# One encoder block on one core: modulation tiles redistributed over the stages, four diagonals for the row of silu(c), and each group's h computed inside the group before

## The chip, the cores and the metric

The kernel runs on one core of one Trainium2 chip. The metric is the time of one execution in microseconds on the device (us); before the change it is 1734.44 us, the median of three runs (1733.49 to 1734.98). Engine names are those of the profile: PE is the matmul engine and PEld its weight loads, DVE the vector engine, ACT the scalar engine, SP the queue that issues the transfers.

## What is computed

```python
mod = silu(c) @ w_ada + b_ada            # six vectors of 2048: sh1, sc1, gt1, sh2, sc2, gt2
h   = rmsnorm(x, g_pre_mix) * (1 + sc1) + sh1
y   = hybrid_mixer(h, ...)               # h @ w_in, a gated recurrence, window attention, w_a, w_b, w_out
x   = x + gt1 * rmsnorm(y, g_post_mix)
h   = rmsnorm(x, g_pre_ffn) * (1 + sc2) + sh2
y   = expert_choice_ffn(h, ...)          # 16 experts, each takes 32 of the 256 tokens
out = x + gt2 * rmsnorm(y, g_post_ffn)
```

There are 256 tokens and 2048 channels, all in float32. The weights make up nearly all of the 630 MB that are read, and each is used once.

## The kernel before

All weights come as tiles of 128 x 2048 floats (1 MB, 8 KB of each partition), and one list sets the order of the whole first part. This list, `prog`, is written out by hand (lines 227 to 264). Its entries are: `X` (load and normalise x), `A` and `B` (one tile of w_ada), `H` (make h for a group of the contraction), `W` (one tile of w_in), `YA`, `YB` and `O` (tiles of w_a, w_b and w_out). The transfers are issued by SP in exactly this order, and the experts' 384 tiles follow in `estream`. Every tile takes the slot that has been free for longest (`Mem.get`); there are 27 slots of 8 KB, four of which form a small ring for split weights (`hring`).

**Modulation.** `expand` (line 288) spreads silu(c), which lies over the partitions, into a row `CR` that every partition holds: for each of four blocks of 512, DVE writes a diagonal matrix (line 282), PE multiplies it by ones, and ACT copies the result (line 293). All four blocks use one buffer `diag`. `ada` (line 390) then multiplies a w_ada tile by `CR` and sums along the row, one DVE instruction per tile (line 392, called an *ada multiply* below). There are 96 of them: 32 `A` tiles (sh1 and sc1, needed for h) and 64 `B` tiles (the other four vectors, needed only in the last stage of the mixer and in the experts).

**Products.** A `W` tile is first split into a high and a low part (`split`: ACT casts in two halves at line 426, DVE subtracts at line 427), and then `prod` runs three products for each of its pieces; `finish` does this one tile behind the split (`LA = LAH = 1`). A tile of kind "t" takes 48 matmuls of 256 columns, one of kind "n" 24 of 512.

**Early groups.** Ten chunks of w_in (`EARLY`) are run in four groups, each over four of the 16 steps of the contraction, so that a group needs only eight `A` tiles. Between groups a chunk's sum is copied out of the accumulator (line 763) and in again (line 760). `("H", g)` stands at the head of each group. There the main loop (line 838) finishes all pending products, and then makes h for the group's four steps in `make_h` (lines 409 to 411, on ACT, ACT and DVE): the first half at once (`HK = 1`), the rest behind the split of the group's first tile. The `A` tiles of group g + 1 are mixed in after the second to the ninth tile of group g; in the last group 8 `B` tiles take their place (`BE = 8`).

**Late chunks, Y and O.** Eleven chunks (`LATE`, 44 tiles) are run one after the other, with 38 `B` tiles mixed in (`BL = 0.87`). Beside them `run_bg` works off the recurrence (`hgrn`, four parts) and then the attention (`attn_pre`, `attn`), four steps of these after each tile. Then come 16 tiles `YA` and `YB` and 16 tiles `O`, with the last 18 `B` tiles after the first 18 of these 32 (`BD = 18`). `router_consts` runs when the 48th `B` tile is done. Last come the router and the 16 experts.

Of the kernel before, what the change touches and what calls it, by code (L numbers as in the profile page):

```python
# [14 lines left out]
F32 = mybir.dt.float32  # L15
# [11 lines left out]
H = 8  # L27
# [3 lines left out]
EPS = 1e-6  # L31
ATT_SCALE = 128 ** -0.5
NEG = -3.0e38
BL = 0.87
BE = 8
BD = 18
NHL = 4
BG = 4
GRP = [4, 4, 4, 4]
NA0 = 1  # L40
HK = 1
LAH = 1


# [81 lines left out]
def block_kernel(ctx: ExitStack, tc: tile.TileContext, x, cols, pos, ident_in, hmask, smask, w_ada, w_in, w_a, w_b, w_out, w_r, w_gu, w_dn, out):  # L126
    nc = tc.nc
    V, S, E = nc.vector, nc.scalar, nc.tensor
# [3 lines left out]
    mem = Mem(sp, 27)  # L132
# [10 lines left out]
    def bank():  # L143
        ring["m"] = (ring["m"] + 1) % 3
        return PS[:, 2048 + 512 * ring["m"]:2560 + 512 * ring["m"]]
# [18 lines left out]
    pairs = []  # L164

    def latest(engine):
        for i in reversed(nc.cur_bb.bb.instructions):
            if i.engine == engine:
                return i
# [8 lines left out]
    def mm(o, l, r, start, stop, **kw):  # L178
        E.matmul(o, l, r, start=start, stop=stop, skip_group_check=True, **kw)  # L179
# [7 lines left out]
    def col(n, a=0, b=None):  # L187
        lo, hi = COLS[n]
        t, o = (ct0, 0) if lo < NCOL0 else (ct, NCOL0)
        return t[:, lo - o + a:(hi if b is None else lo + b) - o]  # L190
# [15 lines left out]
    def tiny(n):  # L206
        a = spos[0]
        spos[0] += n
        assert spos[0] <= SMW
        return small[:, a:a + n]  # L210

    def table(name="natural_log_exp_and_others"):

        S.preload_act_table_set(name)

    def rsqrt(ss, n):

        l, r, t, v = tiny(n), tiny(n), tiny(n), tiny(n)
        S.activation(l, ss, AF.Ln, scale=1.0 / D, bias=epsc)
        S.activation(r, l, AF.Exp, scale=-0.5)  # L220
        V.tensor_scalar(v, ss, 1.0 / D, EPS, ALU.mult, ALU.add)
        V.tensor_tensor(t, r, r, ALU.mult)
        V.scalar_tensor_tensor(t, t, -0.5, v, ALU.mult, ALU.mult)
        V.scalar_tensor_tensor(r, t, 1.5, r, ALU.add, ALU.mult)
        return r


    NG = len(GRP)
    G0 = [sum(GRP[:g]) for g in range(NG)]
    prog = [("X",)]  # L230
    a_tiles = [("A", p, k) for k in range(KT) for p in range(2)]
    b_tiles = [("B", p, k) for p in range(2, 6) for k in range(KT)]
    prog += a_tiles[:2 * GRP[0]]
    for g in range(NG):
        prog.append(("H", g))
        if g < NG - 1:
            todo = a_tiles[2 * G0[g + 1]:2 * G0[g + 1] + 2 * GRP[g + 1]]
        else:
            todo = b_tiles[:BE]
            b_tiles = b_tiles[BE:]  # L240
        nt, ne = len(todo), len(EARLY)
        for i, n in enumerate(EARLY):
            prog.append(("W", n, G0[g], GRP[g]))
            k = min(nt, (i + 1) * nt // (ne - NA0)) - min(nt, i * nt // (ne - NA0))
            prog += todo[:k]
            todo = todo[k:]
        prog += todo
    def mix(items, n, m):

        nonlocal prog, b_tiles  # L250
        n = min(n, len(b_tiles))
        for i, it in enumerate(items):
            prog.append(it)
            k = min(n, (i + 1) * n // m) - min(n, i * n // m)
            prog += b_tiles[:k]
            b_tiles = b_tiles[k:]

    late = [("W", n, 4 * q, 4) for n in LATE for q in range(4)]
    mix(late, int(BL * len(late) + 0.5), len(late))
    dlist = []  # L260
    for c in range(4):
        dlist += [("YA", c, q) for q in range(2)] + [("YB", c, q) for q in range(2)]
    dlist += [("O", c, q) for c in range(4) for q in range(4)]
    mix(dlist, len(b_tiles), BD)

# [14 lines left out]
    def spread(c4, w, b=None):  # L280

        V.tensor_tensor(w, ident[:, None, :].to_broadcast([128, 4, 128]),
                        c4[:, :, None].to_broadcast([128, 4, 128]), ALU.mult)
        b = bank() if b is None else b
        mm(b, ones, w.rearrange("p a b -> p (a b)"), True, True)
        return b

    def expand(c16, name):

        r = mem.get([D], F32, name)  # L290
        w = mem.get([4, 128], F32, "diag")
        for c in range(4):
            S.copy(r[:, 512 * c:512 * c + 512], spread(c16[:, 4 * c:4 * c + 4], w))  # L293
        mem.put(w)
        return r

# [5 lines left out]
    def hk(tl, kt):  # L302
        return tl[kt // 8][:, kt % 8, :]
# [3 lines left out]
    S.activation(sig, col("c"), AF.Sigmoid)  # L307
    V.tensor_tensor(sig, sig, col("c"), ALU.mult)
    CR = expand(sig, "crow")
    X = [mem.get([D], F32, "x") for _ in range(NT)]  # L310
    ssq = tiny(NT)

    def norm_x():
        for tt in range(NT):
            nc.sync.dma_start(X[tt], x[tt])
        scr = mem.get([D], F32, "sq")
        for tt in range(NT):
            S.activation(scr, X[tt], AF.Square, accum_out=ssq[:, tt:tt + 1])
        mem.put(scr)
        rs = rsqrt(ssq, NT)  # L320
        for k2 in range(8):
            if k2 % 2 == 0:
                for tt in range(NT):
                    xp = X[tt][:, 256 * k2:256 * k2 + 512]
                    S.activation(xp, xp, AF.Copy, scale=rs[:, tt:tt + 1])
            b = bank()
            for j in range(2):
                for tt in range(NT):
                    E.transpose(b[:, 256 * j + 128 * tt:256 * j + 128 * tt + 128],
                                X[tt][:, 128 * (2 * k2 + j):128 * (2 * k2 + j) + 128], ident)  # L330
            S.copy(NTl[k2 // 4][:, 2 * (k2 % 4):2 * (k2 % 4) + 2, :].rearrange("p a b -> p (a b)"), b)
        mem.put(*X)

# [56 lines left out]
    def ada(p, k, t):  # L390

        V.scalar_tensor_tensor(t, t, 1.0, CR, ALU.mult, ALU.mult, accum_out=MOD[:, p, k:k + 1])  # L392
        mem.put(t)

    def mod_gain(p, ks):
        m = MOD[:, p, ks]
        V.tensor_tensor(m, m, bada[:, p, ks], ALU.add)
        if p in (1, 4):
            V.scalar_tensor_tensor(m, m, 1.0, col("gpm" if p == 1 else "gpf")[:, ks], ALU.add, ALU.mult)
        elif p in (2, 5):  # L400
            V.tensor_tensor(m, m, col("gqm" if p == 2 else "gqf")[:, ks], ALU.mult)

    def make_h(g):
        ks = slice(G0[g], G0[g] + GRP[g])
        mod_gain(0, ks)
        mod_gain(1, ks)
        for kt in range(ks.start, ks.stop):
            n = hk(NTl, kt)
            S.activation(n, n, AF.Identity, scale=MOD[:, 1, kt:kt + 1], bias=MOD[:, 0, kt:kt + 1])
            S.copy(hk(HH, kt), n)  # L410
            V.tensor_tensor(hk(HL, kt), n, hk(HH, kt).bitcast(F32), ALU.subtract)
            if kt % 2:
                yield
        if g == NG - 1:
            mem.put(*NTl)
# [57 lines left out]
    def late_tiles(names):  # L473
        for n in names:
            OT[n] = mem.get([8, 256], F32R, n)
# [149 lines left out]
    def attn_pre():  # L625
        AQ, AKV = SL["AQ"], SL["AKV"]
        late_tiles(("BH", "BL"))
        V.memset(SC, NEG)
# [15 lines left out]
    def attn(h):  # L644
# [40 lines left out]
        S.copy(OT["BH"][:, h, :], b[:, :256])  # L685
        V.tensor_tensor(OT["BL"][:, h, :], b[:, :256], OT["BH"][:, h, :].bitcast(F32), ALU.subtract)
        yield
# [6 lines left out]
        "YA": (lambda k: OT["OH"][:, k, :], lambda k: OT["OL"][:, k, :]),  # L694
        "YB": (lambda k: OT["BH"][:, k, :], lambda k: OT["BL"][:, k, :]),
        "O": (lambda k: hk(MH, k), lambda k: hk(ML, k)),
# [51 lines left out]
    def finish(it, parts):  # L748
# [32 lines left out]
        elif k in ("YA", "YB"):  # L781
# [10 lines left out]
            if q == 1:  # L792
# [6 lines left out]
                else:  # L799
# [8 lines left out]
                    if c == 3:  # L808
                        table()
                        mem.put(OT["OH"], OT["OL"], OT["BH"], OT["BL"])  # L810
        else:
# [22 lines left out]
    last_b = [it for it in prog if it[0] == "B"][-1]  # L834
    LA = LAH
    pend = []
    hs = iter(())
    for it in prog:
        if it[0] == "H":
            while pend:  # L840
                finish(*pend.pop(0))
            hs = make_h(it[1])
            for _ in range(HK):
                next(hs)
            continue
        if it[0] == "X":
            norm_x()
            rotary()
            continue
        t = take()  # L850
        if it[0] in "AB":
            ada(it[1], it[2], t)
            if it[0] == "B" and it[2] % 4 == 3:
                mod_gain(it[1], slice(it[2] - 3, it[2] + 1))
            if it == last_b:
                mem.put(CR)
            if it == ("B", 4, KT - 1):
                router_consts()
        else:
            pend.append((it, split(t)))  # L860
            for _ in hs:
                pass
            while len(pend) > LA:
                finish(*pend.pop(0))
            run_bg(BG)
# [117 lines left out]
    for e in range(NE):  # L983
# [9 lines left out]
        for k in range(KT):  # L993
            w = take()
# [201 lines left out]
```

## Time and profile before

| | us |
|---|---|
| three runs: lowest, median, highest | 1733.49, 1734.44, 1734.98 |
| the profiled execution, its own time | 1734.13 |
| its span, first to last instruction | 1732.4 |
| PE, DVE, ACT busy | 1440.0, 777.0, 554.2 |
| read from HBM | 630.04 MB, 365 GB/s over the span |

A view by windows gives, for each stretch of the span, its length, the busy time of each engine with the number of its instructions, the granted clock of PE as a share of 2.4 GHz (PEclk; 0.50 is the lower level, 1.2 GHz), the busy share of the 16 DMA engines, and the rate. The time line lists instructions by start and duration, runs of equal ones merged (x2), with the idle time ahead of them and what ended it in brackets. Matmuls overlap one another, so PE's busy time is no measure of its pace.

### The profile page before, as it was taken

Reading aid. Unit: us, or ns where it says so; the run is one execution under the profiler, and the core shown is the slowest. Engines: PE = TensorE matmul, PEld = TensorE weight load, DVE = VectorE, ACT = ScalarE, POOL = GpSimd, SP = SyncE. Lnnn points to the kernel's source line nnn. Section 1 sums busy time; section 2 is a strip of 40 time slices with the busy share of each in tenths; the row PEclk is TensorE's granted clock in tenths of the full one; section 3 lists DMA queues with packets and bytes.
Section 4 is the critical chain, followed back from the end, with each engine's and each line's share of the span. In section 5 each row is a group of like instructions: output and inputs, shape, how many; then the busy total and the mean of one; then the engine's idle time right before and its main releaser. Section 6 shows DMA issues by size and latency. Waiting matters only on the chain.

```text
span 1732.4 us, 24211 instructions
## 1 busy us (share of the span) xinstructions
PE 1440.0 (83%) x10234; PEld 920.8 (53%) x10234; DVE 777.0 (45%) x1056; ACT 554.2 (32%) x854; POOL 0.2 (0%) x4
## 2 busy tenths in 40 slices
PE   4999999999999999997977767776777777777677
PEld 2989998789999999872422212321222222222123
DVE  6777787999997898443111101111111111111013
ACT  6467776665574444431200100000010000001013
POOL 0000000000000000000000000000000000000000
PEclk8999999999999999998998988888888887889797
DMA  9988955776978889867999999999999999999996
GB/s 384 418 342 320 361 209 217 275 298 247 355 305 341 336 349 371 334 249 292 419 419 420 419 419 419 419 419 419 419 420 420 419 419 419 420 419 419 419 420 243
DMA packets 88668, 633.72 MB, mean 366 GB/s; under 512 B 10096, under 2 KB 10480, under 8 KB 11760
## 3 DMA queue, kind: packets, MB, share of 16 engines
q1 hardware_dynamic: 88128, 631.39, 90.3%
q8 instruction: 80, 1.31, 0.3%
q10 hardware_dynamic: 432, 0.79, 0.1%
q14 instruction: 28, 0.23, 0.0%
HBM read 630.04 MB, written 2.10 MB: 365 GB/s over the span
## 4 chain that ended last, share of the span: by engine, by line
PE 48%; DMA 40%; DVE 6%; ACT 3%; issue 2%; SPq 0%; ACTq 0%; DVEq 0%
PE PS L179 47%; DMA w<-in_w_gu_dram 32%; DMA w<-in_w_dn_dram 7%; DVE w L392 2%; DVE hl L427 1%; ACT ew L1037 1%; DMA w<-in_w_in_dram 1%; ACT hl L426 0%; PE PS L1010 0%; DMA w<-in_w_ada_dram 0%; ACT ew L1007 0%; DVE F L500 0%; PE PS L889 0%; PE PS L678 0%; DVE T L506 0%
## 5 line engine op out<-in xcount | busy, mean ns | idle before, releaser
L179 PE MATMUL PS<-w,rt 128*32 128x512 f32 x2048 | 331.9, 724 | 149.7 <-DMA w<-in_w_gu_dram 148.3
L179 PE MATMUL PS<-hh,hl 128*128 128x256 f32 x2048 | 384.6, 288 | 13.8 <-ACT hl L426 8.9
L179 PE MATMUL PS<-hl,hl 128*128 128x256 f32 (+1 forms) x1184 | 357.0, 302 | 0.0
L179 PEld LDWEIGHTS PS<-hh,hl 128*128 128x128 f32 x2048 | 325.9, 194 | 16.3 <-ACT hl L426 9.3
L427 DVE TENSOR_TENSOR hl<-w,hl 128x1024 fp32r<-128x1024 f32 x232 | 281.4, 1223 | 117.3 <-ACT hl L426 117.0
L426 ACT CAST hl<-w 128x1024 fp32r<-128x1024 f32 x232 | 241.1, 1048 | 162.2 <-PE PS L179 155.0
L179 PEld LDWEIGHTS PS<-w,rt 128*32 128x32 f32 x2048 | 54.2, 117 | 387.6 <-DMA w<-in_w_gu_dram 329.7
L179 PEld LDWEIGHTS PS<-hl,hl 128*128 128x128 f32 x1184 | 229.1, 193 | 7.3 <-issue 1.0
L392 DVE SCALAR_TENSOR_TENSOR w<-w,crow 128x2048 f32<-128x2048 f32 x96 | 218.9, 2285 | 5.3 <-ACT crow L293 2.8
L179 PE MATMUL PS<-ew,rt 128*128 128x256 f32 x512 | 151.8, 422 | 59.8 <-ACT ew L1037 59.8
L1048 DVE TENSOR_TENSOR acc<-acc,PS 128x512 f32<-128x512 f32 x120 | 82.5, 688 | 258.6 <-PE PS L179 258.6
L179 PEld LDWEIGHTS PS<-ew,rt 128*128 128x128 f32 x512 | 91.5, 198 | 131.2 <-ACT ew L1037 117.8
L179 PE MATMUL PS<-w,ew 128*32 128x256 f32 x2048 | 146.9, 407 | 13.9 <-DVE ew L1016 13.9
L1037 ACT COPY ew<-PS 128x256 f32<-128x256 f32 x128 | 47.5, 371 | 250.9 <-PE PS L179 250.9
L1016 DVE TENSOR_TENSOR ew<-ew,PS 128x256 f32<-128x256 f32 x16 | 6.7, 421 | 234.4 <-ACT ew L1015 234.4
L949 DVE TENSOR_SCALAR rt<-ct,rt,small 128x32 f32<-128x32 f32 x32 | 9.4, 301 | 212.8 <-PE PS L179 212.8
L179 PE MATMUL PS<-hl,hh 128*128 128x512 f32 x320 | 101.8, 395 | 3.3 <-DVE hl L427 3.3
L179 PEld LDWEIGHTS PS<-w,ew 128*32 128x32 f32 x2048 | 56.1, 114 | 82.9 <-issue 44.0
L955 ACT COPY ew<-PS 128x512 f32<-128x512 f32 x15 | 8.8, 585 | 281.7 <-PE PS L179 281.7
L1007 ACT COPY ew<-PS 128x512 f32<-128x512 f32 x16 | 9.4, 585 | 235.6 <-PE PS L179 235.6
L179 PE MATMUL PS<-hl,mh 128*128 128x512 f32 x256 | 81.1, 397 | 0.8 <-ACT hl L426 0.7
L179 PEld LDWEIGHTS PS<-hl,hh 128*128 128x128 f32 x320 | 59.3, 188 | 17.0 <-DVE hl L427 5.0
(240 smaller groups left out, 1188.4 us busy)
## 6 DMA issues: line engine op xcount, KB each, us to landing
w<-in_w_gu_dram SPq DMA_DIRECT2D x256, 1024.0 KB, 19.9
w<-in_w_dn_dram SPq DMA_DIRECT2D x128, 1024.0 KB, 19.9
w<-in_w_ada_dram SPq DMA_DIRECT2D x96, 1024.0 KB, 7.2
w<-in_w_in_dram SPq DMA_DIRECT2D x84, 1024.0 KB, 7.3
w<-in_w_out_dram SPq DMA_DIRECT2D x16, 1024.0 KB, 9.2
w<-in_w_a_dram SPq DMA_DIRECT2D x8, 1024.0 KB, 6.4
w<-in_w_b_dram SPq DMA_DIRECT2D x8, 1024.0 KB, 7.6
x<-in_x_dram SPq DMA_DIRECT2D x4, 1024.0 KB, 6.1
```

Of the source, the lines that this page charges most:

```text
L179: E.matmul(o, l, r, start=start, stop=stop, skip_group_check=True, **kw)
L392: V.scalar_tensor_tensor(t, t, 1.0, CR, ALU.mult, ALU.mult, accum_out=MOD[:, p, k:k + 1])
L426: S.copy(hl[:, 0, :], w)
L427: V.tensor_tensor(hl[:, 1, :], w, hl[:, 0, :].bitcast(F32), ALU.subtract)
L949: V.tensor_scalar(oh[:, tt, :], io, pm3[:, tt, e:e + 1], r2[:, tt:tt + 1], ALU.is_equal, ALU.mult)
L955: S.copy(g, b)
L1007: S.copy(gu, b)
L1016: V.tensor_tensor(he, sl_, b3[:, :, 64:128], ALU.mult)
L1037: S.copy(EW[:, 2, 256 * (cb % 2):256 * (cb % 2) + 256], b[:, :256])
L1048: V.tensor_tensor(acc(cb), acc(cb), p3, ALU.add)
```

## The change

The list is built anew, the row of silu(c) gets four diagonal buffers, and h of the next group is made two steps at a time while the last two tiles of the group before are split.

```diff
-BL = 0.87
-BE = 8
-BD = 18
+BE = [0, 4, 4, 12]
+BL = 16
+BD = 27
-NA0 = 1
-HK = 1
+NA0 = 2
+NH0 = 3
...
     for g in range(NG):
-        prog.append(("H", g))
+        todo = b_tiles[:BE[g]]
+        b_tiles = b_tiles[BE[g]:]
         if g < NG - 1:
-            todo = a_tiles[2 * G0[g + 1]:2 * G0[g + 1] + 2 * GRP[g + 1]]
-        else:
-            todo = b_tiles[:BE]
-            b_tiles = b_tiles[BE:]
+            todo = a_tiles[2 * G0[g + 1]:2 * G0[g + 1] + 2 * GRP[g + 1]] + todo
         nt, ne = len(todo), len(EARLY)
         for i, n in enumerate(EARLY):
             prog.append(("W", n, G0[g], GRP[g]))
+            if g == 0 and i == 0:
+                prog.append(("H", 0))
             k = min(nt, (i + 1) * nt // (ne - NA0)) - min(nt, i * nt // (ne - NA0))
             prog += todo[:k]
             todo = todo[k:]
+
+            if g < NG - 1 and i == ne - NH0:
+                prog.append(("H", g + 1))
...
-    mix(late, int(BL * len(late) + 0.5), len(late))
+    mix(late, BL, len(late))
...
-        w = mem.get([4, 128], F32, "diag")
+        w = mem.get([4, 4, 128], F32, "diag")
         for c in range(4):
-            S.copy(r[:, 512 * c:512 * c + 512], spread(c16[:, 4 * c:4 * c + 4], w))
+            S.copy(r[:, 512 * c:512 * c + 512], spread(c16[:, 4 * c:4 * c + 4], w[:, c]))
...
     CR = expand(sig, "crow")
+    crow_done = latest(mybir.EngineType.Activation)
...
             S.activation(scr, X[tt], AF.Square, accum_out=ssq[:, tt:tt + 1])
+        pairs.append((latest(mybir.EngineType.Activation), crow_done))
...
-    hs = iter(())
+    hs, hg_ = iter(()), 0
     for it in prog:
         if it[0] == "H":
-            while pend:
-                finish(*pend.pop(0))
-            hs = make_h(it[1])
-            for _ in range(HK):
-                next(hs)
+            hs, hg_ = make_h(it[1]), it[1]
+            if it[1] == 0:
+                n, p = len(nc.cur_bb.bb.instructions), latest(mybir.EngineType.Activation)
+                for _ in hs:
+                    pass
+                pairs += [(i, p) for i in nc.cur_bb.bb.instructions[n:] if i.engine == mybir.EngineType.Activation]
             continue
...
             pend.append((it, split(t)))
-            for _ in hs:
-                pass
+            if it[0] == "W" and it[2] < G0[hg_]:
+                next(hs, None)
+            else:
+                for _ in hs:
+                    pass
```

`pairs` holds orderings within an engine: the first of a pair is placed behind the second. So the second square of x stands behind the last copy of `CR`, and the first group's h behind the casts of its first `W` tile.

Written out, the list has these numbers of w_ada tiles beside each stage's product tiles:

| stage (product tiles) | before | after |
|---|---|---|
| ahead of group 0 | 8 A | 8 A |
| groups 0, 1, 2, 3 (10 each) | 8 A, 8 A, 8 A, 8 B | 8 A, 8 A + 4 B, 8 A + 4 B, 12 B |
| late chunks (44) | 38 B | 16 B |
| YA and YB (16) | 16 B | 16 B |
| O (16) | 2 B | 12 B |

In the groups after the change the w_ada tiles follow the first eight product tiles, none the last two. Of the first 22 late tiles (the stretch in which the recurrence runs) 19 had a `B` tile before, and 8 have one after. The 48th `B` tile stands behind the second `YA`/`YB` tile before, and behind the twelfth after; the last one frees `CR` in stage O both times, behind its second tile before and its eleventh after.

## Rows read from the trace of the kernel before

**Rows 1.** Windows by stage: length, PE, PEld, DVE, ACT, POOL busy, PEclk, DMA share, GB/s.
```profile
104.00:277.00 173.00, 173.00 (x1300) 167.21 (x1301) 129.35 (x128) 127.70 (x144) 0.00 (x0) 0.99 0.79 302
277.00:441.00 164.00, 156.93 (x1027) 137.28 (x1026) 158.55 (x221) 97.41 (x133) 0.00 (x0) 0.99 0.68 257
441.00:518.00 77.00, 77.00 (x589) 74.19 (x589) 73.02 (x122) 49.08 (x100) 0.00 (x0) 1.00 0.83 321
588.00:688.00 100.00, 99.24 (x795) 96.93 (x794) 88.56 (x89) 42.95 (x43) 0.00 (x0) 1.00 0.92 362
688.00:773.00 85.00, 84.23 (x362) 67.60 (x362) 38.57 (x35) 34.24 (x44) 0.00 (x0) 1.00 0.76 294
...
720.00:763.00 43.00, 43.00 (x185) 34.39 (x184) 20.98 (x20) 19.56 (x25) 0.00 (x0) 1.00 0.56 194
790.00:805.00 15.00, 6.82 (x30) 2.23 (x34) 9.72 (x33) 1.33 (x4) 0.00 (x0) 0.56 0.26 108
...
850.00:1732.00 882.00, 641.22 (x4624) 216.82 (x4619) 133.94 (x236) 85.17 (x220) 0.00 (x0) 0.86 0.99 411
```

**Rows 2.** Time line of the start, all engines: from the first diagonal to the first product.
```profile
5.09 2.07 PE L179 MATMUL PS<-diag,ones 128*128 128x512 f32 x2 [5.09 <-DVE diag L282]
...
16.75 0.58 ACT L293 COPY crow<-PS 128x512 f32<-128x512 f32 x1 [2.33 <-PE PS L179]
...
17.37 2.29 DVE L392 SCALAR_TENSOR_TENSOR w<-w,crow 128x2048 f32<-128x2048 f32 x1 [2.77 <-ACT crow L293]
...
33.92 2.28 DVE L392 SCALAR_TENSOR_TENSOR w<-w,crow 128x2048 f32<-128x2048 f32 x1
...
36.70 1.09 ACT L409 ACTIVATE nT<-nT,MOD 128x256 f32<-128x256 f32 x2 [5.57 <-DVE MOD L399]
37.70 0.69 ACT L410 CAST hh<-nT 128x256 fp32r<-128x256 f32 x2
...
38.30 1.99 ACT L426 CAST hl<-w 128x1024 fp32r<-128x1024 f32 x2
...
39.39 0.58 PE L179 MATMUL PS<-hh,hl 128*128 128x256 f32 x1 [8.88 <-ACT hl L426]
```

**Rows 3.** DMA issues: the eighth w_ada tile and the first w_in tiles, issue and landing.
```profile
10.23 0.33 SPq L160 DMA_DIRECT2D w<-in_w_ada_dram  x1
...
w<-in_w_ada_dram SPq DMA_DIRECT2D x1, 1024.0 KB, 19.9
...
12.73 2.82 SPq L160 DMA_DIRECT2D w<-in_w_in_dram  x2
...
w<-in_w_in_dram SPq DMA_DIRECT2D x1, 1024.0 KB, 19.9
```

**Rows 4.** ACT's time line: groups 0 to 1 (99 to 118 us), then 1 to 2.
```profile
99.61 1.01 ACT L763 COPY Q<-PS 128x1024 f32<-128x1024 f32 x1
...
102.72 1.96 ACT L760 COPY PS<-F 128x1024 f32<-128x1024 f32 x2
...
111.31 1.01 ACT L763 COPY F<-PS 128x1024 f32<-128x1024 f32 x1 [1.89 <-PE PS L179]
...
157.04 1.01 ACT L763 COPY Q<-PS 128x1024 f32<-128x1024 f32 x1
...
162.48 1.02 ACT L763 COPY Q<-PS 128x1024 f32<-128x1024 f32 x1 [0.97 <-PE PS L179]
...
168.24 1.02 ACT L763 COPY F<-PS 128x1024 f32<-128x1024 f32 x1 [1.82 <-PE PS L179]
```

**Rows 5.** PE in the recurrence: products of 512 columns, then all matmuls touching the recurrence's tiles.
```profile
L179 PE MATMUL PS<-hl,hh 128*128 128x512 f32 x191 | 61.5, 399 | 3.3 <-DVE hl L427 3.3
...
L179 PE MATMUL PS<-hl,hl 128*128 128x512 f32 x95 | 38.0, 400 | 0.0
...
277.00:441.00 164.00, 33.85 (x248) 26.34 (x248) 42.29 (x92) 37.80 (x64) 0.99 0.68 257
```

## The prediction

> **What bounds the kernel now.** I read the windows by stage first, then the time line where a stage begins late, then matmul counts where a stage is slow. From 850 us to the end the DMA engines are 99% busy: the experts' transfers set the pace there, and the change does not touch them [rows 1]. From 790 to 805 us, while the router is worked out, DMA is only 26% busy: all free slots hold experts' tiles, and no slot comes free until PE starts on expert 0. So the end is the time at which PE gets there plus a fixed transfer, and whatever PE saves ahead of 805 us comes off the end one for one, as long as the slots are full by then.
>
> Ahead of that PE is the bound. From 104 to 277 us it is busy without a gap, likewise from 441 to 518 us, and nearly so from 588 to 773 us [rows 1]. Three places lose time. First the start: the first product begins at 39.39 us [rows 2]. Second the step from group 0 to group 1: the copies out of the accumulator stand 11.70 us apart (99.61 to 111.31 us), whereas from group 1 to 2 a tile of 512-column products takes 5.44 us and the next group's first tile 5.76 us, with nothing lost [rows 4]. Third the recurrence (277 to 441 us): DVE is busy for 158.55 of 164 us, and PE waits for it in turn [rows 1].
>
> **The change part by part.**
>
> *Start.* Four diagonal buffers take DVE's wait for PE out of the making of CR. From the first matmul pair at 5.09 us, four of 2.07 us back to back end at 13.4 us, and the last copy (0.58 us) at 14.0 us; now it ends at 17.3 us, with the first ada multiply at 17.37 us [rows 2]. The second square of x no longer stands between the copies. Seven multiplies and the small work between them take 33.92 − 17.37 = 16.55 us, so the eighth would start at 30.5 us. Its tile lands at 10.23 + 19.9 = 30.1 us [rows 3], just in time, and more could not be won. From there to h it is 36.70 − 33.92 = 2.8 us [rows 2]: the modulations are there at 33.3 us. The first w_in tile lands at 12.73 + 19.9 = 32.6 us [rows 3]; its casts (1.99 us [rows 2]), now put ahead of h, end at 34.6 us. One step of h is half of 1.09 and of 0.69 us [rows 2], which gives a first product at 35.5 us against 39.39 us, 3.9 us earlier. I take 3.5, because the low part of h now queues on DVE behind two subtractions. Bounds: 0, if the casts come later and hold up h, to 4.
>
> *From group 0 to group 1.* 11.70 − 5.76 = 5.9 us are lost [rows 4]. The chain is ACT's: h's casts, the second tile's casts and the copies back in (102.72 us) stand behind the copy out at 99.61 us, because the eighth A tile is multiplied only behind the split of the ninth tile. After the change the A tiles end one product tile earlier, nothing is flushed, and h is made behind the splits of the last two tiles. The step from group 1 to 2 shows that this suffices even with the old order. I take 5.9 (0 to 5.9). At the two later steps there is nothing to win.
>
> *Groups 1 to 3 get 12 more ada multiplies.* 12 x 2.29 = 27.5 us of DVE time. DVE goes from 129.35 to 156.8 of 173 us, 91% [rows 1]. Cover: PE. From 441 to 518 us DVE is busy for 73.02 of 77 us (95%) with PE gapless, and from 588 to 688 us for 88.56 of 100 us with PE at 99.24 [rows 1]. Transfers: at 411 GB/s a tile takes 2.55 us [rows 1]; 22 tiles in a group take 56.1 us, and PE needs 8 x 5.76 + 2 x 5.44 = 57.0 us. It fits, barely. I take a loss of 1 us; bounds 0 to 27.5, the case in which nothing is covered.
>
> *Late chunks lose 22.* In the recurrence it is 11 (19 less 8): 11 x 2.29 = 25.2 us of DVE, from 158.55 to 133 us [rows 1]. What this gives is what PE loses there now. In that window PE ran 191 + 95 = 286 matmuls of 512 columns, which is 11.9 tiles at 5.44 us, or 64.8 us. Of the 1027 matmuls 248 touch the recurrence's tiles; the remaining 493 are 10.3 tiles at 5.76 us, or 59.2 us [rows 1, 4, 5]. The 248 have a busy time of 33.85 us, the most that they can have held PE; their weight loads sum to 26.34 us, which I take as the least [rows 5]. So PE needed 150 to 158 of the 164 us, and lost 6 to 14. I take the middle, 10, and assume that nothing of it remains, since DVE would be at 133 of about 154 us (86%), below the 95% beside which PE has no gap. Bounds 0 to 14. The other 11 removed tiles lie beside a gapless PE and give nothing.
>
> PE's busy time reads differently: 156.93 of 164 us [rows 1] would leave 7.1 us to win, and the sum would come out at 1720. The Trainium skill (Perfetto Trace Analysis, Identifying the Most-Contended Engine) says that matmul busy time is no good measure, since these instructions are pipelined, and that weight-load busy time is better. The trace agrees: weight loads fall from 167.21 of 173 us to 137.28 of 164 us, far more than busy time does.
>
> *Stage O gets 10 more.* 22.9 us of DVE on 38.57 of 85 us makes 72% [rows 1]; cover: PE. Their transfers are 10 x 2.55 = 25.5 us; DMA idles for 0.44 x 43 = 19 us from 720 to 763 us and for 0.74 x 15 = 11 us from 790 to 805 us [rows 1], so 30 us take them in. The last B tile holds CR, one slot, for nine O tiles longer. The router's constants move by ten tiles with their few small DVE operations. I take 1 us; bounds 0 to 14, the part of the 25.5 us that only the last 11 would absorb.
>
> **Sum.** −3.5 − 5.9 − 10 + 1 + 1 = −17.4 us. The profiled execution took 1734.13 us, its span and 1.7 us around it, so 1716.7 us; the median of the runs stands 0.3 us above it: **1717.0 us**.
>
> **Rivals.**
> *(A) The recurrence stays slow.* It is a chain through DVE, ACT and PE in order; if its latency and not DVE's load holds PE, 0 to 3 of the 10 us come, and the time is 1724 to 1727 us. For it: PE is idle only 7 us there by its busy time. Against: attention, worked off in the same way from 441 us on, costs no gap with DVE at 95% [rows 1].
> *(B) The tiles moved early cost more than they save.* DVE takes its work in order. Rows 4 show ACT do so: the copies back in wait at 102.72 us behind casts. If a B tile of groups 1 to 3 has not landed when DVE reaches its multiply, the subtractions behind it wait, and PE behind those. Price: up to 12 x 2.29 = 27.5 us, hence 1716.7 − 1 + 27.5 = 1743 us, slower. It decides once more than 18.4 of the 27.5 us show up on PE, which needs DMA to lose its lead within group 1. The Trainium skill (TensorE: Matmul & The Clock Gate, the section on the array's architectural detail) calls ACT and DVE strictly first in, first out, which is this mechanism. Against: group time exceeds transfer time, even if by only 1 us.
> *(C) Stage O gives it back.* The 24 slots of expert 0 are not full when PE arrives, for 10 B tiles stand ahead of them: 14 us return, 1730.7 us. Against: 30 us of idle DMA.
> That a part does nothing is covered by the zero bounds of the start and of the step to group 1: if h still came late, 5.9 us would be missing, at 1723 us.
>
> **How the numbers follow.** A measurement of this kernel can tell about 0.2% (3.5 us) from no change. My forecast with all its terms near their values (1710 to 1723 us) has 0.70; (A) 0.14; (C) and other part losses between 1731 and 1737 us 0.08; (B) 0.08. Faster by over 0.2% are the first two: 0.84; same 0.08; slower 0.08. The range: the sum with every term at its best is 1734.1 − 4 − 5.9 − 14 = 1710 us, and I go to 1709; upward it takes in (A) at 1727, so 1728. Outside it are (B), (C) and a little more, under 0.2.
>
> **What would show it.** First product near 35.5 us; two copies out 5.8 us apart at the first step between groups; the recurrence stage with DVE below 90% and shorter by 10 us; stages Y and O as long as before; DMA idle for some us just ahead of expert 0. PE gaps that wait for DVE's subtraction in groups 1 to 3 would speak for (B); PE gaps in the recurrence for (A); an unbroken DMA up to expert 0 for (C).

## The result and the profile after

The changed kernel takes **1763.4 us** (median of four runs, 1762.53 to 1765.52) against 1733.97 us before (1733.38 to 1734.98) on the same chip: a ratio of 1.0172 [1.016, 1.0185], slower by 29 us. Forecast were 1717.0 us and a range of 1709 to 1728 us. The profiled execution has a span of 1762.0 us, 29.6 us longer than before.

The windows show where. They are cut at the copies out of the last tile of group 0 and of group 3, at the copy of the last late chunk and at the end of stage O, so that each holds the same work in both kernels. First the kernel before (columns as in [rows 1]):

```profile
99.60:276.80 177.20, 173.01 (x1299) 167.26 (x1300) 132.07 (x132) 131.89 (x149) 0.00 (x0) 0.99 0.80 305
276.80:587.30 310.50, 303.43 (x2189) 280.83 (x2188) 286.59 (x396) 179.98 (x266) 0.00 (x0) 0.99 0.76 288
587.30:773.10 185.80, 184.17 (x1162) 165.22 (x1161) 127.86 (x126) 77.92 (x87) 0.00 (x0) 1.00 0.85 331
```

The same stages after, then the stretch ahead of expert 0 and the experts:

```profile
94.40:311.70 217.30, 189.54 (x1304) 177.69 (x1303) 155.28 (x158) 131.70 (x147) 0.00 (x0) 0.93 0.80 312
311.70:615.40 303.70, 300.87 (x2185) 278.80 (x2184) 243.75 (x343) 179.35 (x266) 0.00 (x0) 1.00 0.62 226
615.40:801.00 185.60, 184.06 (x1162) 165.18 (x1160) 147.24 (x149) 77.82 (x86) 0.00 (x0) 1.00 0.93 374
819.00:834.00 15.00, 6.60 (x38) 2.14 (x42) 9.72 (x33) 1.46 (x5) 0.00 (x0) 0.66 0.36 148
878.00:1760.00 882.00, 644.93 (x4636) 220.29 (x4628) 134.25 (x237) 85.30 (x220) 0.00 (x0) 0.85 0.99 411
```

Groups 1 to 3 grew from 177.2 to 217.3 us, although the step from group 0 to 1 that they contain became shorter. The late chunks fell by 6.8 us, Y and O stayed. Ahead of expert 0 the DMA engines still idle (36% busy; 26% in [rows 1]), and the experts run at the same 411 GB/s. So the whole loss lies in groups 1 to 3.

The start came as worked out [rows 2]: the first ada multiply at 13.98 us, the casts as soon as the tile has landed, the first product at 35.78 us (forecast 35.5). From the time line of all engines:

```profile
13.98 2.29 DVE L397 SCALAR_TENSOR_TENSOR w<-w,crow 128x2048 f32<-128x2048 f32 x1
...
32.45 1.99 ACT L431 CAST hl<-w 128x1024 fp32r<-128x1024 f32 x2 [4.71 <-DMA w<-in_w_in_dram]
...
35.78 0.79 PE L179 MATMUL PS<-hh,hl 128*128 128x256 f32 x2 [8.66 <-ACT hh L415]
```

ACT's time line answers to [rows 4]. L768 is the copy out, L765 the copy in, L431 the cast (L763, L760 and L426 before):

```profile
94.45 1.01 ACT L768 COPY Q<-PS 128x1024 f32<-128x1024 f32 x1 [1.61 <-PE PS L179]
...
100.20 1.02 ACT L768 COPY F<-PS 128x1024 f32<-128x1024 f32 x1 [1.93 <-PE PS L179]
...
111.72 1.02 ACT L768 COPY F<-PS 128x1024 f32<-128x1024 f32 x1 [1.77 <-PE PS L179]
112.77 1.02 ACT L765 COPY PS<-Q 128x1024 f32<-128x1024 f32 x1
117.48 1.01 ACT L768 COPY F<-PS 128x1024 f32<-128x1024 f32 x1 [3.69 <-PE PS L179]
118.52 1.02 ACT L765 COPY PS<-Q 128x1024 f32<-128x1024 f32 x1
119.47 3.88 ACT L431 CAST hl<-w 128x1024 fp32r<-128x1024 f32 x4
128.44 1.02 ACT L768 COPY Q<-PS 128x1024 f32<-128x1024 f32 x1 [5.09 <-PE PS L179]
```

The step from group 0 to 1 is right: 94.45 to 100.20 us is 5.75 us, where 11.70 us stood before. But from 117.48 to 128.44 us one tile takes 11.0 us. ACT is free from 113.8 us on and does nothing for 3.69 us: the next instruction in its queue is the copy out of the tile that PE is still multiplying. Only behind that copy, and behind the copy in, stand the casts of the tile that PE needs next; then the casts of two tiles come at once. The tile was not late. It was issued at 88.23 us and took 15.5 us to land, so it lay there from 103.7 us, and its cast starts at 119.47 us (SP's time line, then the DMA view of this issue):

```profile
88.23 0.33 SPq L160 DMA_DIRECT2D w<-in_w_in_dram  x1
```

```profile
w<-in_w_in_dram SPq DMA_DIRECT2D x1, 1024.0 KB, 15.5
```

The view of waits, for PE from 100 to 300 us, shows the same nine times:

```profile
PE PS L179 <- ACT hl L431: 26.3, 9, 3.3
PE PS L179 <- DVE hl L432: 1.2, 4, 0.4
```

They are one tile each of the chunks q0, hg0 and v0 in each of the groups 1 to 3. DVE's subtractions, on which rival (B) rested, cost 1.2 us in all; DVE itself waits for the casts (4.72 us ahead of its subtraction at 120.54 us) and, by the view of its waits, never for a transfer in these groups:

```profile
115.74 0.08 DVE L397 DVE_READ_ACCUMULATOR w<-w,crow 128x1 f32 x1
120.54 2.36 DVE L432 TENSOR_TENSOR hl<-w,hl 128x1024 fp32r<-128x1024 f32 x2 [4.72 <-ACT hl L431]
```

Why a wait of 3 us makes a tile 5.2 us longer stands on PE's time line and in two windows around it:

```profile
117.04 0.28 PE L179 MATMUL PS<-hl,hl 128*128 128x256 f32 x1
117.16 0.28 PE L179 MATMUL PS<-hh,hl 128*128 128x256 f32 x1
120.56 0.40 PE L179 MATMUL PS<-hh,hl 128*128 128x256 f32 x1 [3.12 <-ACT hl L431]
120.79 0.39 PE L179 MATMUL PS<-hl,hl 128*128 128x256 f32 x1
```

```profile
94.40:118.00 23.60, 23.04 (x193) 22.84 (x191) 19.31 (x18) 14.31 (x15) 0.00 (x0) 1.00 1.01 418
118.00:124.00 6.00, 3.22 (x14) 2.92 (x15) 3.46 (x3) 5.32 (x6) 0.00 (x0) 0.73 1.02 422
```

Ahead of the wait the matmuls start 0.12 us apart, behind it 0.2 us and more; the granted clock is 0.73 over these 6 us, a mean between the lower level (0.50, 1.2 GHz) and the upper (1.00, 2.4 GHz), after 1.00 in the stretch before, in which PE had no gap up to this wait.

My reading at this point: the kernel's program fixes the order of ACT's instructions when it is built, from the list and from `pairs`, and the new list made it put nine tiles' casts behind the copy out of the tile before. The rivals: that the 12 additional ada multiplies or their transfers cost the time (load), or that the tiles' new places do so in some other way.

### The profile page after: what moved, and what is told of

It is laid out like the page before. It is cut to its first block, busy times and chain, and to the rows that moved or that the text cites. A ratio compares the mean times of both kernels' runs of the same rounds, so it can differ in the third digit from the quotient of the medians.

```text
span 1762.0 us, 24234 instructions
## 1 busy us (share of the span) xinstructions
PE 1451.8 (82%) x10234; PEld 931.6 (53%) x10234; DVE 778.5 (44%) x1056; ACT 554.6 (31%) x854; POOL 0.2 (0%) x4
## 4 chain that ended last, share of the span: by engine, by line
DMA 47%; PE 44%; DVE 4%; ACT 3%; issue 2%; SPq 0%; ACTq 0%; DVEq 0%
PE PS L179 42%; DMA w<-in_w_gu_dram 33%; DMA w<-in_w_dn_dram 11%; DMA w<-in_w_in_dram 2%; DVE hl L432 1%; DMA w<-in_w_ada_dram 1%; ACT hl L431 1%; ACT ew L1046 0%; DVE w L397 0%; DVE F L505 0%; PE PS L898 0%; PE PS L1019 0%; PE PS L683 0%; ACT ew L1016 0%; ACT PS L765 0%
## 5 line engine op out<-in xcount | busy, mean ns | idle before, releaser
L179 PE MATMUL PS<-w,rt 128*32 128x512 f32 x2048 | 324.1, 711 | 146.3 <-DMA w<-in_w_gu_dram 144.8
L179 PE MATMUL PS<-hh,hl 128*128 128x256 f32 x2048 | 388.9, 290 | 29.1 <-ACT hl L431 19.1
L431 ACT CAST hl<-w 128x1024 fp32r<-128x1024 f32 x232 | 237.9, 1047 | 167.9 <-PE PS L179 156.6
L179 PE MATMUL PS<-w,ew 128*32 128x256 f32 x2048 | 151.3, 418 | 15.4 <-DVE ew L1025 15.4
L179 PE MATMUL PS<-hl,hh 128*128 128x512 f32 x320 | 106.5, 409 | 8.1 <-ACT hl L431 7.2
L958 DVE TENSOR_SCALAR rt<-ct,rt,small 128x32 f32<-128x32 f32 x32 | 9.4, 300 | 217.3 <-PE PS L179 217.3
```

Source lines behind the costliest of these rows:

```text
L431: S.copy(hl[:, 0, :], w)
L958: V.tensor_scalar(oh[:, tt, :], io, pm3[:, tt, e:e + 1], r2[:, tt:tt + 1], ALU.is_equal, ALU.mult)
```

## The experiments

"Groups 1 to 3" is always the time from the copy out of group 0's last tile to that of group 3's, "late chunks" from there to the copy of the last late chunk.

**e_order: the changed kernel, ACT's order put right.** Each copy out of an early tile is held behind the casts of the next tile.

```diff
             pend.append((it, split(t)))
+            cast = latest(mybir.EngineType.Activation)
...
             while len(pend) > LA:
-                finish(*pend.pop(0))
+                done = pend.pop(0)
+                finish(*done)
+                if done[0][0] == "W" and done[0][1] in EARLY:
+                    pairs.append((latest(mybir.EngineType.Activation), cast))
```

> The changed kernel, with one thing added: in the early groups the copy out of the accumulator of a tile is placed behind the casts of the next tile, as it was before the change. Transfers, multiplies and matmuls are the same. If ACT's order is the cause (nine product tiles in groups 1 to 3 whose casts stand behind the copy-out of the tile before; 10.96, 11.20 and 9.71 us between copies out instead of 5.76), all nine gaps close and some 46 us go: 1717 us (1710 to 1724). If DVE's 12 more multiplies are the cause, or the transfers of 22 tiles in a group, nothing changes: 1758 us or more.

Measured: 1723.6 us (1720.45 to 1724.0), ratio to before 0.9939 [0.9924, 0.9953], at the upper end of the expected 1710 to 1724. Nothing but the order differs from the changed kernel, and 40 us are gone. ACT's time line at the same place, then PE's waits from 95 to 275 us:

```profile
112.78 1.02 ACT L768 COPY F<-PS 128x1024 f32<-128x1024 f32 x1 [1.77 <-PE PS L179]
113.82 1.02 ACT L765 COPY PS<-Q 128x1024 f32<-128x1024 f32 x1
114.78 1.99 ACT L431 CAST hl<-w 128x1024 fp32r<-128x1024 f32 x2
118.53 1.01 ACT L768 COPY F<-PS 128x1024 f32<-128x1024 f32 x1 [1.76 <-PE PS L179]
```

```profile
PE PS L179 <- ACT hl L431: 1.8, 2, 0.9
```

The casts now stand between the copies, and the copies out come 5.75 us apart. Groups 1 to 3 take 176.1 us where the changed kernel takes 217.3.

**e_bad_order: the kernel before, with the wrong order alone.** The list is that of before; at those nine tiles the tile ahead is finished first, and the casts are held behind its copy out.

```diff
-            pend.append((it, split(t)))
+            if it[0] == "W" and it[1] in ("q0", "hg0", "v0") and it[2] >= 4:
+                while pend:
+                    finish(*pend.pop(0))
+                done, n = latest(mybir.EngineType.Activation), len(nc.cur_bb.bb.instructions)
+                pend.append((it, split(t)))
+                pairs += [(i, done) for i in nc.cur_bb.bb.instructions[n:] if i.engine == mybir.EngineType.Activation]
+            else:
+                pend.append((it, split(t)))
```

> The kernel before, with no tile moved; only the casts of nine product tiles (q0, hg0 and v0 of groups 1 to 3) are placed behind the copy-out of the tile before. If ACT's order is the cause, PE waits at each of them for at least that copy and one cast (1.0 us each), and more where its clock falls: 2 to 5 us each, 18 to 45 us in all, 1752 to 1779 us. If DVE's load or the transfers are the cause, nothing is lost: 1734 us, within 4 us.

Measured: 1765.53 us (1764.24 to 1766.58), ratio 1.0184 [1.0169, 1.0199]. The order alone, without a single ada multiply moved, gives the loss. PE's waits from 100 to 300 us name the same cause and count:

```profile
PE PS L179 <- ACT hl L426: 18.6, 9, 2.3
```

**e_shift_only: the kernel before, with the tiles redistributed alone** (`BE`, `BL` and `BD` of the change and the loop that uses them; h and the start as before).

```diff
-BL = 0.87
-BE = 8
-BD = 18
+BL = 16
+BE = [0, 4, 4, 12]
+BD = 27
```

> The kernel before with only the B tiles spread as after the change (0, 4, 4, 12 in the groups, 16 late, 28 at the end); one diagonal buffer, h at the head of its group, as before. In this program six product tiles of groups 1 to 3 have their casts behind the copy-out of the tile before (hg0 and v1 of each). If that order is the cause, six gaps of some 5 us are lost and some 7 us won in the recurrence: 1757 us (1745 to 1765). If DVE's load or the transfers are the cause, the loss is that of the changed kernel, 46 us less 7: 1773 us.

Measured: 1759.26 us (one run). Here too the loss is there. The six tiles of the expectation (hg0 and v1 of each group), and no others after the step into group 1, stand 10.6 to 12.7 us behind the tile before, where a step without loss takes 5.4 to 5.8, and PE's waits from 100 to 300 us name the casts. The new list is what brings the order about.

```profile
PE PS L179 <- ACT hl L426: 16.0, 5, 3.5
```

**e_noshift: the changed kernel with the tiles where they were** (start and h as changed).

```diff
-BE = [0, 4, 4, 12]
-BL = 16
-BD = 27
+BE = [0, 0, 0, 8]
+BL = 38
+BD = 18
```

> The changed kernel with the numbers of B tiles of before (8 in the last group, 38 beside the late chunks, 18 at the end): the four diagonals, the new place of h and the A tiles one product tile earlier remain. Under each theory the nine gaps are gone, because no product tile has two w_ada tiles ahead of it. What it tells is the sum of the start (5.2 us in the trace after) and the step from group 0 to 1 (5.9 us) alone: 1734 - 11 = 1723 us (1719 to 1728). If those two are given back later, 1734 us.

Measured: 1728.5 us (1726.45 to 1730.83), ratio 0.9969 [0.9959, 0.9979], just above the expected 1719 to 1728. One step of 12.6 us is left, at the last tile of group 1, by the time line again a matter of order: this time the copy *in* of that tile (149.80 us) stands behind the copy out of the tile ahead and the casts of the one behind. ACT's time line there, and PE's waits from 95 to 275 us:

```profile
147.00 1.01 ACT L768 COPY Q<-PS 128x1024 f32<-128x1024 f32 x1 [0.65 <-PE PS L179]
147.91 1.99 ACT L431 CAST hl<-w 128x1024 fp32r<-128x1024 f32 x2
149.80 1.02 ACT L765 COPY PS<-Q 128x1024 f32<-128x1024 f32 x1
```

```profile
PE PS L179 <- ACT PS L765: 3.9, 1, 3.9
```

**e_diag: the kernel before with the start alone** (the diff's hunks on the diagonals, `crow_done` and the pair of the second square).

> The kernel before with the four diagonals alone, and the second square of x behind the copies of the row of silu(c). The ada multiplies start 3 to 4 us earlier, but the first product waits for the first w_in tile's casts behind h. If the start is carried to the end one for one: first product 36 to 37 us and 1731 us (1730 to 1733). If something later swallows it: 1734.

Measured: 1729.93 us (1729.37 to 1731.44), ratio 0.9978 [0.9969, 0.9987], just below the expected 1730 to 1733. The first product comes at 35.8 us, 3.6 us earlier, and the end 4.2 us earlier: what the start wins is carried to the end.

**e_best and e_noshift_in: the copies in, too.** In `finish`, each chunk's sum is copied in right behind the copy out of the tile two places ahead, and the pair of e_order takes `cur["out"]`.

```diff
-                if not first:
+                if not first and not cur.pop((n, k0), False):
                     S.copy(ps, s)
...
+                cur["out"] = latest(mybir.EngineType.Activation)
+                nx = EARLY.index(n) + 2
+                n2, k2 = EARLY[nx % 10], k0 + 4 * (nx // 10)
+                if 0 < k2 < KT:
+                    S.copy(ps, slab(n2))
+                    cur[n2, k2] = True
```

> The changed kernel with ACT's order put right as in e_order, and in addition each chunk's sum copied in again right behind the copy-out of the tile two places ahead of it, so that no copy-in stands behind casts. Order theory: what e_order still lost in groups 1 to 3 (58.9, 58.9 and 58.3 us where 57 were worked out, with two steps of 7.4 us) shrinks by 1 to 5 us: 1719 to 1723 us against e_order's 1723.6. If the remaining loss is DVE's or the transfers' (12 more ada multiplies in these groups), it stays: 1723 to 1725 us.

> Start and h as in the changed kernel, B tiles where they were before, ACT's order and copies in as in e_best. The step of 12.6 us at the last chunk of group 1 in e_noshift should be gone if it was the copy-in behind casts: 1728.5 less 5 to 7, 1721 to 1724 us. The distance to e_best is what the redistribution of the tiles is worth under a right order: 3 to 7 us if the late chunks' gain (6.7 us in e_order) is kept, 0 if the groups give it back.

Measured: e_best 1721.05 us (1720.6 to 1723.87), ratio 0.9928 [0.9915, 0.994]; e_noshift_in 1723.6 us (1722.21 to 1725.34), 0.994 [0.9925, 0.9955]. In e_noshift_in groups 1 to 3 fell to 172.2 us, with no step longer than 6.8 us, and the late chunks take 308.1 us. In e_best it is 176.1 and 303.4 us: the redistribution wins 4.7 us late and gives back 3.9 us early. The two steps of 7.4 us that e_order had are still there, so the copies in were not their cause. The times of e_best and e_order overlap: the copies in brought nothing that these runs can tell.

**e_bfirst: B tiles ahead of A tiles** in groups 1 and 2 (`todo` put ahead of `a_tiles[...]`), otherwise e_best.

> e_best with one line turned round: in groups 1 and 2 the four B tiles stand ahead of the eight A tiles and not behind them. In e_best the eighth A multiply ends at the sixth product tile, and h's 3.3 us of ACT stand there, in the middle of a group, ahead of the next tile's casts (one step of 7.4 us). If that is what e_best still loses in groups 1 and 2 (58.9 us each), they come to 57 to 57.5 us, as in e_noshift_in, and the time to 1717 to 1719 us. If the loss is the load of 12 multiplies or of 22 transfers per group, they stay at 58.9 and the time at 1721.

Measured: 1721.58 us (1720.08 to 1723.58), ratio 0.993 [0.9917, 0.9942]: no gain. The groups still take 58.7 us each; the steps of 7.4 us became steps of 8.2 us two tiles further on, where h's operations had gone. By the expectation this speaks for load; what the time line shows there is h waiting 2.66 us for its modulations on ACT, with casts behind it. The run did not settle it.

**e_h_behind: e_best, with h's ACT operations held behind the casts.**

```diff
             if it[0] == "W" and it[2] < G0[hg_]:
+                n = len(nc.cur_bb.bb.instructions)
                 next(hs, None)
+                pairs += [(i, cast) for i in nc.cur_bb.bb.instructions[n:] if i.engine == mybir.EngineType.Activation]
```

> e_best, and h's ACT operations of the next group are held behind the casts of the tile whose split they follow in the program, so that they cannot move to the middle of a group. If the step of 7.4 us in groups 1 and 2, which neither the early copy-in (e_best) nor the turned list (e_bfirst) removed, is still a matter of ACT's order, these groups come to 57.0 to 57.5 us and the time to 1717 to 1719 us. If it is the load of 12 more ada multiplies, groups 1 and 2 stay at 58.7 to 58.9 us and the time at 1721.

Measured: **1717.75 us** (1717.17 to 1718.72), ratio 0.9902 [0.9888, 0.9916], the fastest of all. e_best's ACT time line, and then the windows of e_h_behind over groups 1 to 3, the late chunks, and Y and O:

```profile
124.48 1.02 ACT L768 COPY Q<-PS 128x1024 f32<-128x1024 f32 x1 [1.76 <-PE PS L179]
...
126.80 1.10 ACT L414 ACTIVATE nT<-nT,MOD 128x256 f32<-128x256 f32 x2 [0.26 <-DVE MOD L404]
...
130.00 1.99 ACT L431 CAST hl<-w 128x1024 fp32r<-128x1024 f32 x2
131.90 1.00 ACT L768 COPY Q<-PS 128x1024 f32<-128x1024 f32 x1
```

```profile
95.50:267.80 172.30, 172.30 (x1303) 166.36 (x1303) 153.78 (x156) 132.95 (x150) 0.00 (x0) 1.00 0.95 390
267.80:571.40 303.60, 300.75 (x2186) 278.75 (x2184) 243.66 (x343) 178.38 (x264) 0.00 (x0) 1.00 0.61 227
571.40:757.00 185.60, 184.02 (x1162) 165.17 (x1160) 147.21 (x149) 77.78 (x86) 0.00 (x0) 1.00 0.93 373
```

In e_best all four steps of h for group 2 (126.80 to 130.00 us) stand in the middle of group 1 ahead of the casts; without that, PE is busy for all 172.30 us of the groups, with the 12 additional multiplies in them and DVE at 153.78 us (89%), DMA at 95%. Groups 1 and 2 take 57.0 us each, as the order theory has it, and all three take what e_noshift_in needs without the 12 multiplies (172.2 us). Load costs nothing there. Against e_noshift_in (1723.6 us) the redistribution is worth some 6 us once the order is right, most of it in the late chunks (303.6 against 308.1 us).

**e_late0: e_order without any B tile beside the late chunks** (`BL = 0`).

> e_order with no B tile at all beside the late chunks; the 16 that stood there stand beside Y and O, where the time will be longer. Read is the length of the late chunks alone: 310.5 us before, 303.8 in e_order with 8 ada multiplies beside the recurrence. If DVE's load is what still holds PE in the recurrence, another 8 multiplies less bring 3 to 6 us more: 298 to 301 us. If it is the recurrence's own chain (rival A), the length stays at 302 to 304 us.

Measured: the late chunks take 304.1 us, against 303.8 in e_order, though DVE is busy for 203.03 us in them and not 243.90. (The whole, 1748.88 us in one run, is longer: Y and O then hold 44 B tiles, and from 576 to 820 us PE waits 15.9 us for DVE's subtractions. There the load does cost.) Fewer multiplies beside the recurrence than the change leaves there bring nothing.

**e_late_tail: e_best with no B tile in groups 1 and 2, 8 beside the recurrence, 16 beside the rest of the late chunks.**

```diff
-BE = [0, 4, 4, 12]
+BE = [0, 0, 0, 12]
...
-    mix(late, BL, len(late))
+    mix(late[:22], 8, 22)
+    mix(late[22:], BL, 22)
```

> e_best with no B tile in groups 0 to 2, 12 in group 3, 8 beside the recurrence's 22 late tiles and 16 beside the other 22 (28 stay for Y and O). If the redistribution's worth lies only in the recurrence having 8 ada multiplies and not 19, the groups take 57.0 us each, the late chunks 303 to 304 us, and the time is 1716 to 1719 us. If the 16 multiplies beside the second half of the late chunks cost there, the late chunks take 305 to 308 us and the time is 1720 to 1724.

Measured: 1721.62 us (1720.98 to 1723.52), ratio 0.9929 [0.9916, 0.9943]. Groups 1 and 2 take 57.0 us each and the late chunks 303.9, as the first theory has it, but the time is the second one's: Y and O take 189.9 us, 4 more. Two windows of e_late_tail there:

```profile
600.00:640.00 40.00, 40.00 (x336) 40.00 (x335) 40.00 (x43) 15.45 (x15) 0.00 (x0) 1.00 0.88 333
640.00:680.00 40.00, 36.90 (x244) 33.31 (x244) 37.17 (x38) 16.24 (x16) 0.00 (x0) 0.96 0.89 347
```

DVE is busy for all of the first 40 us, and in the next 40 PE falls behind. In e_best, where the stage begins 4.3 us later, DVE is at 36.60 us in the first window and PE at 39.23 us in the second. That DVE's backlog causes it was not tried by itself, and PE's waits do not settle it: in this stage they are 1.7 us for a cast on ACT and 1.4 us for a subtraction on DVE, against 0.7 us for a cast in e_best.

## Why the prediction was wrong

In us, change of the span against before, by stage:

| term | forecast | changed kernel | e_order | e_h_behind |
|---|---|---|---|---|
| start, to the end of group 0 | −3.5 | −5.2 | −4.1 | −4.1 |
| step to group 1, and groups 1 to 3 | −5.9 + 1 | **+40.1** | −1.1 | −4.9 |
| late chunks | −10 | −6.8 | −6.7 | −6.9 |
| Y and O | 0 | −0.2 | −0.1 | −0.2 |
| from there to the end | +1 | +1.7 | +1.2 | +0.6 |
| sum | −17.4 | +29.6 | −10.8 | −15.5 |

**The step that failed** is "Groups 1 to 3 get 12 more ada multiplies", for which I took a loss of 1 us with bounds of 0 and 27.5 us; 46 us came (the 40.1 us of the table, and the 5.9 us of the step to group 1 that were won in the same row). It named PE as the cover and weighed the load of DVE and of the transfers. Both were weighed rightly: e_h_behind holds the same multiplies and transfers, and PE has no gap. What it did not price is that a new list makes a new order on ACT as well, an engine that in this stretch is busy for only 131.70 of 217.3 us. Against e_h_behind the groups are 217.3 − 172.3 = 45.0 us longer, of which 27.5 us are PE's waits in the trace (26.3 for casts, 1.2 for DVE). Nearly all the rest is PE's own pace: for the same matmuls it is busy for 189.54 us and not 172.30, at a granted clock of 0.93 and not 1.00. e_order and e_bad_order show the cause from both sides. Even the upper bound (all of DVE's 27.5 us exposed) was too low: it was a price of the load that was moved, and e_bad_order shows a loss of this size with no load moved.

**Rival (B)** had the sign, the place and PE's gaps right, and the wrong engine: PE was to wait for subtractions behind a B tile that had not landed. The waits on DVE are 1.2 us, and the B tiles were not the ones late. What it took from the Trainium skill (TensorE: Matmul & The Clock Gate, the array's architectural detail), that ACT and DVE are strictly first in, first out, is what happened on ACT: 3.69 us of idle ACT with a landed tile waiting behind a copy that could not start. I had seen ACT's order at work in [rows 4] and did not ask what the change would do to it.

**The late chunks** are a term mis-sized: 6.8 us came, not 10, near the lower end of the 6 to 14 us that I had worked out. Rival (A), that the recurrence's own chain holds PE, was priced at 0 to 3 us won and did not come so. By the windows above PE is not busy for 7.1 us of the late chunks before and for 2.8 us after, so by busy time little was left to win, and e_late0 shows that a lighter DVE wins nothing more. Whether the chain of (A) holds these last 2.8 us is not shown; e_late0's 304.1 us are what its expectation gave for (A). The reading by PE's busy time, which would have left 7.1 us and which I set aside, was the nearer one here, against what I had drawn from the Trainium skill (Perfetto Trace Analysis, Identifying the Most-Contended Engine), whose sentence is on how close a kernel is to roofline and not on the size of a gap. The fall of the weight loads that I read as agreement came mostly from the mix of products and not from lost time: after the change PE is busy for nearly the whole recurrence, and its weight loads still take only 134.75 of 156 us, since a tile of 512-column products has half the matmuls, and so half the weight loads, of the other kind.

```profile
312.00:468.00 156.00, 153.29 (x1019) 134.75 (x1018) 142.59 (x204) 96.34 (x132) 0.00 (x0) 1.00 0.58 214
```

DVE is at 91% there, where the forecast had below 90%.

**The start** (first product at 35.78, forecast 35.5), **the step to group 1** (5.9 us, gone) and **stages Y and O** came as worked out. That the start's row shows 5.2 and 4.1 us where the first product came only 3.6 us earlier lies in group 0's first tile, for which the forecast had no term: it ran from 39.39 to 48.39 us at a granted clock of 0.66 before, from 35.78 to 43.22 us at 0.79 after. Rival (C) fell: DMA idles ahead of expert 0 after as before. With ACT's order put right everywhere, the forecast's own sum is nearly met: 1717.75 us measured, 1717.0 forecast. Part of that is luck: in the span 15.5 of the 17.4 us came, with 3.1 us too little in the late chunks and 0.6 us too much at the start.

Open is why the program's ordering step chose these places: it was not examined, only that the list alone brings it about (e_shift_only) and that a few forced orderings cure it. The lists give a hint. The 12 w_ada tiles of a group, spread over eight places, put two of them ahead of f1, q0, hg0 and v0 in groups 1 to 3, and three of these four are the tiles that lost; spread over nine places in e_shift_only, they stand ahead of b1, hg0 and v1, and the last two lost. Before the change and in e_noshift no product tile of these groups has two ahead of it, and in neither does PE wait for a cast in these groups. No run tried this by itself.

## What to carry to other kernels

Where an engine's order is made anew whenever a list changes, cost a move not by load alone: for each engine that runs in order, write down which instruction will stand ahead of the one that the bound engine needs next, also where the engine is far from full. In the profile the sign is an idle engine, a landed input and a copy out ahead of the input's first instruction. If the order matters, force it in the code; here one such ordering turned 1763 us into 1724 us (e_order), and with the copies in moved and h held back it was 1718 us.

## What the runs showed that was not expected

A short wait of PE costs more than itself: nine waits of 26.3 us in total stretched the groups by 45 us, with the granted clock at 0.73 in the 6 us around one of them and matmuls 0.2 us apart and more behind it, where 0.12 us stood ahead. In e_bad_order 18.6 us of waits for casts, and 4.4 us of other waits more than before, stretched the groups by 35.7 us (from 177.2 to 212.9). But there the waits for casts are 2.05 to 2.3 us, and the clock did not fall behind each: over the nine long steps it is 0.73 to 0.83 in four and 1.00 in five, while in the changed kernel it is 0.82 to 0.85 in all nine. Two of e_bad_order's steps, columns as in [rows 1]:

```profile
211.21:221.52 10.31, 7.80 (x50) 7.60 (x51) 7.22 (x9) 7.59 (x14) 0.00 (x0) 0.83 0.68 268
281.88:290.72 8.84, 6.31 (x50) 6.10 (x51) 8.49 (x8) 4.77 (x6) 0.00 (x0) 1.00 0.60 206
```
